# A half tile of tokens multiplied with one joint operand, and a reordered norm ahead of the first layer's routing

## The chip, the cores and the metric

The kernel runs on one core of a Trainium2 chip. The metric is device time in microseconds (us), the median of three runs. The core has five engines that run side by side, each through its own queue in order: TensorE (PE, with its weight loads shown as PEld), VectorE (DVE), ScalarE (ACT), GpSimd (POOL), and SyncE (SP), which here only starts DMA transfers. Matrix products land in PSUM, which has 8 banks of 512 float32 columns over 128 partitions.

## What is computed

Two layers of a hybrid backbone over 512 latent tokens (D = 1024) with 256 context tokens. Each layer has a token mixer (three parallel head groups, an output projection, a gated residual) and then a retrieval step (PEER). The change touches the seam between the two and the retrieval's last matrix product:

```python
x = x + g1 * yx                                   # output projection, gated residual
hx = rmsnorm(x, norm2_g[l]) * (1.0 + sc2) + sh2   # second norm
x = x + g2 * peer(hx, ...)

def peer(h, wq, keys, u_tab, v_tab):              # per token: 8 heads x top-16 of 128^2 experts
    q = (xb @ wq).reshape(T, PEER_HEADS, PEER_DQ)
    ...                                           # two top-k over 128 keys, one over 256 pairs
    gate = jax.nn.softmax(top_s, axis=-1)
    act = jax.nn.gelu(jnp.einsum('td,thkd->thk', xb, u_tab[eid]))
    return jnp.einsum('thk,thkd->td', gate * act, v_tab[eid])
```

The first layer also does all this for the context; the second does it for the latent tokens alone.

## The kernel before

The retrieval is done in two ways at once. **Dense**: for the first T latent tokens (T = 384 in the first layer, 320 in the second) all 16384 experts are computed. A u block (`ublock`) is 128 experts against T tokens, on PE, with a GELU on ACT into a slot of the SBUF tiles `PA` and `PB`. `weights` builds the sparse gate matrix by one-hot matmuls (`pwt`) and multiplies it into the slots. A v block (`vblock`, 128 per layer) multiplies a slot with 128 rows of `peer_v` and accumulates over all blocks in PSUM (`dacc0`, `dacc1`, ...). **Gathered**: for the other tokens (in the second layer 128 + 64, in the first 128 latent tokens and the 256 of the context) the rows of the chosen experts are fetched by an indirect DMA of POOL (`rows_of`, L1123), 128 rows of 1024 numbers at a time into one of five buffers `grow`, and DVE multiplies and adds each (L1134, L1147). There are 768 such gathers in the first layer and 384 in the second.

To keep the accuracy of float32, PE products are done in parts: an operand is split into a rounded part (`h`, a cast on ACT, L113) and the remainder (`l`, a subtraction on DVE, L114), and `mm` (L121) issues three passes. A v block loads its 128 x 1024 rows into a raw tile `uv` (three buffers in the second layer, shared with u blocks, two in the first), and splits them into `uvh` and `uvl` (two buffers each). The slot's columns are split into `wh` and `wl`.

T = 320 is two and a half tiles of 128 tokens. The half tile is not split: L1292 multiplies 64 float32 columns of the slot with the raw `uv`, one half of D into PSUM partitions 0 to 63 and the other into 64 to 127 of one bank, 64 of PE's columns each.

The order of the work on each engine is fixed when the kernel is built, by a planner that steps through a model of the machine: when an engine is idle in it, the ready instruction of the lowest level number goes next. `self.prio(n)` sets the level. The first layer's latent mixer and its retrieval have 3, the second layer's retrieval 5, all gathers 6, so that gathers fill what the rest leaves open on DVE. Within a level the order of the program text decides. On the chip each engine then works through its list in order and waits by semaphores.

At the seam, `back` runs the output projection tile by tile (`pwo`, two PSUM slots `S` of two banks), DVE scales and adds the residual (L610, L616), and SP stores the sum (L617). `transposed`, called by `route` (L944), squares and normalises a tile (L421, `rstd`, L423), transposes it by eight matmuls (`ptr`, L441, in one-bank slots `w`), scales it on the way out (L454, L456), and splits it into `dhT`. Then come the routing matmuls (`ppq`, `psc`) and the first u blocks (`pst`). In the first layer the pool that holds `ptr` is laid over banks of the projection's `S` slots; the transposes of the score maps in the mixer (`bpt`) use the last two banks.

Of the kernel before, what the change touches and what calls it, by code (L numbers as in the profile page):

```python
# [9 lines left out]
F32 = mybir.dt.float32  # L10
# [5 lines left out]
ALU = mybir.AluOpType  # L16
# [55 lines left out]
class Kern:  # L72
# [101 lines left out]
    def schedule(self):  # L174
        a = self.a
        with ExitStack() as er:
            ec = ExitStack()
            self.context(ec, 0)
            with self.banks("ctx0", "right", w=2, S=1) as ps, ExitStack() as e0:
                md = e0.enter_context(self.pool("mod", side="right"))  # L180
                pm = e0.enter_context(self.banks("mod", "right", w=1))
                fl = e0.enter_context(self.pool("flt"))
                pf = e0.enter_context(self.banks("flt", "left", w=2, S=1))
                with self.prio(1), ExitStack() as e:
                    self.filters(fl, pf, 0, LC)
                    self.modulation(md, pm, 0, 0, 2)
                    st = self.front(e, ps, ps, 0, 1, 1, side="right")
                    self.filters(fl, pf, 0, LX)
                    self.modulation(md, pm, 0, 2, 6)
                    self.back(ps, ps, 0, 1, st, None)  # L190
                    self.filters(fl, pf, 1, LX)
                    self.modulation(md, pm, 1, 0, 2)
            self.gp = er.enter_context(self.pool("gath", side="right"))
            with self.prio(1), self.banks("rc", "right", w=2) as ps:
                gc = self.route(ps, 0, 1, "GG", side="right")
            with self.banks("x0", "left", w=2, S=2) as ps:
                with ExitStack() as e:
                    with self.prio(3):
                        pr = e.enter_context(self.banks("x0b", "right", w=2))
                        st = self.front(e, ps, pr, 0, 0, 3, split=False)  # L200
                        ex, keep = ExitStack(), ExitStack()
                        rn = self.back(ps, pr, 0, 0, st, ex, keep=keep)
                        ex = (keep, ex)
                ec.close()
            with self.prio(6):
                self.gtile_u(0, gc[0])
                self.gtile_v(0, 1, 0, gc[0])
                self.gtile_u(0, gc[1])
            with self.prio(3):
                gx, ex = self.peer_x(0, 384, 31, 33, (36, 46, 46), ex, rn)  # L210
            with self.prio(6):
                self.gtile_u(0, gx[3])
                self.gtile_v(0, 0, 3, gx[3])
                self.gtile_v(0, 1, 1, gc[1])
            with ExitStack() as ec, ExitStack() as e:
                self.context(ec, 1)
                ps = e.enter_context(self.banks("x1", "left", w=2, S=2))
                pr = e.enter_context(self.banks("x1b", "right", w=2))
                with self.prio(3):
                    st = self.front(e, ps, pr, 1, 0, 4, ctx=True)  # L220
                with self.prio(4):
                    self.back(ps, pr, 1, 0, st, None, (2, 6))
            with self.prio(5):
                gx, _ = self.peer_x(1, 320, 32, 46, (44, 42, 42), (ex,))
            with self.prio(6):
                for i in sorted(gx, reverse=True):
                    self.gtile_u(1, gx[i])
                    self.gtile_v(1, 0, i, gx[i])
# [689 lines left out]
    def route(self, ps, l, s, kinds, hT=None, iT=None, i2n=None, side="left", done=(), fill=iter(()), rn=None,  # L918
# [10 lines left out]
        with ExitStack() as es:  # L929
# [10 lines left out]
            with nullcontext(rn) if rn else self.pool(f"rn{l}{s}", side=side) as sp:  # L940
                A2, B2 = rows or [sp.tile([128, D], F32, name=n) for n in ("A2", "B2")]
                nc.sync.dma_start(A2, bcast_rows(self.rows[l, 2, s, :]))
                nc.sync.dma_start(B2, bcast_rows(self.rows[l, 1, s, :]))
                for i, x in enumerate(self.transposed(sp, ps, l, 1, s, range(nt), hT, rest)):  # L944
                    if kinds[i] == "D":
                        continue
                    outs[i] = h = gp.tile([128, D], F32, name="ghx", bufs=2)
                    for dst, src in ((LO, HI), (HI, HI)) if kinds[i] == "H" else ((ALL, ALL),):
                        nc.vector.tensor_mul(h[dst], x[src], A2[src])
                        nc.vector.tensor_add(h[dst], h[dst], B2[dst])  # L950
# [233 lines left out]
    def peer_x(self, l, T, nA, nB, widths, done, rn=None):  # L1184
# [13 lines left out]
        with ExitStack() as es:  # L1198
# [74 lines left out]
                                                   1.0 / GSCALE, dst, op0=ALU.mult, op1=ALU.mult)  # L1273

            def vblock(i, sp):
                r0 = l * NEXP + i * 128
                if i in plain:
                    raw = dn.tile([128, D], F32, name="uv", bufs=2 + l)
                    nc.sync.dma_start(raw, a["peer_v"][r0:r0 + 128, :])
                    v, w = [raw], [slot(i)]  # L1280
                else:
                    raw, v = block("v", a["peer_v"][r0:r0 + 128, :])
                    w = [sp.tile([128, nd * 128], F32R, name=n, bufs=2) for n in ("wh", "wl")]
                    self.split(*w, slot(i)[:, :nd * 128])
                vh = [[x[:, h * 512:(h + 1) * 512] for x in v] for h in range(2)]
                for t in range(nd):
                    for h in range(2):
# [1 line left out]
                                [vh[h]], i == 0, i == 127)  # L1289
                if half:  # L1290
                    for h in range(2):
                        nc.tensor.matmul(acc[nd][h * 64:(h + 1) * 64], slot(i)[:, nd * 128:T],  # L1292
                                         raw[:, h * 512:(h + 1) * 512], start=(i == 0), stop=(i == 127))

            fill = (ublock(i) for i in range(nA))
            with self.banks(f"r{l}", "right", w=2, S=2) as ps:
                gx = self.route(ps, l, 0, "D" * nd + "H" * (nt - nd) + "G" * (4 - nt), hT, iT, i2n, "right", done, fill,
                                rn, [free[:, (i - 2) * D:nA * T + (i - 1) * D] for i in range(2)] if rn else None)
            for _ in fill:
# [2 lines left out]
            sp = ew.enter_context(self.pool(f"dw{l}"))  # L1302
            if nB:
                P.append(sp.tile([128, nB, T], F32, name="PB"))
            pa = es.enter_context(self.banks(f"da{l}", "left", w=nt - nd, S=nd))
            acc = [pa.S(f"dacc{i}") if i < nd else pa.w(f"dacc{i}") for i in range(nt)]
            due = {}
            for c, w in enumerate(widths):
                m0, m1 = cuts[c + 1] - R, cuts[c]
# [11 lines left out]
            if l == 0:  # L1321
                ex = ExitStack()
                self.res[0] = ex.enter_context(self.pool("xs1", side="right")).tile([128, 4, D], F32, name="xs")
            g2, fg, *rest = (free[:, i * D:(i + 1) * D] for i in range(2 + 2 * nt))
            nc.sync.dma_start(g2, bcast_rows(self.rows[l, 3, 0, :]))
            if l:
                nc.sync.dma_start(fg, bcast_rows(a["final_g"]))
# [3 lines left out]
            for t in range(nt):  # L1331
# [1 line left out]
                if t < nd:  # L1333
                    nc.vector.tensor_mul(y, acc[t], g2)
                else:
                    for h in range(2):
                        nc.vector.tensor_mul(y[LO, h * 512:(h + 1) * 512], acc[t][h * 64:(h + 1) * 64],
                                             g2[h * 64:(h + 1) * 64, h * 512:(h + 1) * 512])
                self.ended(dn, l, 0, t, ALL if t < nd else LO, y, res, res if l else self.res[0][:, t, :], fg)
        return gx, ex  # L1340

# [126 lines left out]
```

## Time and profile before

| | us |
|---|---|
| median of three runs (4218.82 to 4229.47) | 4218.94 |
| profiled execution | 4229.7 |
| its span, first to last instruction | 4227.9 |

Busy shares of the span: PE 88%, PEld 66%, DVE 83%, ACT 45%, POOL 37%. Each row of the views below is one execution on the chip, times from the start of the span. An engine's row in the order-of-time view gives start, duration, engine (a "q" for a queue that only issues), source line, operation, output <- inputs, shapes, how many were merged, and in brackets how long the engine was idle before and what it waited for. PE's durations overlap, since matmuls are pipelined: the step from one start to the next is what counts.

### The profile page before, as it was taken

Reading aid. Unit: us, or ns where it says so; the run is one execution under the profiler, and the core shown is the slowest. Engines: PE = TensorE matmul, PEld = TensorE weight load, DVE = VectorE, ACT = ScalarE, POOL = GpSimd, SP = SyncE. Lnnn points to the kernel's source line nnn. Section 1 sums busy time; section 2 is a strip of 40 time slices with the busy share of each in tenths; the row PEclk is TensorE's granted clock in tenths of the full one; section 3 lists DMA queues with packets and bytes.
Section 4 is the critical chain, followed back from the end, with each engine's and each line's share of the span. In section 5 each row is a group of like instructions: output and inputs, shape, how many; then the busy total and the mean of one; then the engine's idle time right before and its main releaser. Section 6 shows DMA issues by size and latency. Waiting matters only on the chain.

```text
span 4227.9 us, 63819 instructions
## 1 busy us (share of the span) xinstructions
PE 3702.5 (88%) x22532; PEld 2806.4 (66%) x22532; DVE 3509.9 (83%) x7455; ACT 1908.9 (45%) x3725; POOL 1543.7 (37%) x1225
## 2 busy tenths in 40 slices
PE   6987987967989999999979889888888999999997
PEld 3645544557878878877547666447788877776654
DVE  5746988888989989988999966645898998898988
ACT  5554343522347536633443344523334745555732
POOL 0000245642344573366447610000225345543243
PEclk7998998978999999999989989899989999999999
DMA  6655687875768897799989942333449888887797
GB/s 208 205 177 179 214 309 247 291 285 196 243 222 271 305 360 256 236 364 353 327 297 345 329 161 83 115 115 102 164 167 353 267 309 288 290 301 281 230 343 273
DMA packets 305634, 1063.74 MB, mean 252 GB/s; under 512 B 35756, under 2 KB 42624, under 8 KB 305314
## 3 DMA queue, kind: packets, MB, share of 16 engines
q0 software_dynamic: 165888, 604.05, 41.2%
q1 hardware_dynamic: 139426, 455.61, 30.7%
q8 instruction: 177, 2.90, 0.3%
q14 instruction: 143, 1.17, 0.1%
HBM read 1042.69 MB, written 16.84 MB: 251 GB/s over the span
## 4 chain that ended last, share of the span: by engine, by line
PE 35%; DMA 21%; DVE 18%; issue 15%; POOL 7%; ACT 5%; SPq 0%; POOLq 0%; DVEq 0%; ACTq 0%
PE pst L121 8%; PE dacc L121 7%; DMA grow<-in_peer_u_dram,eid 7%; POOL grow L1123 7%; DMA uv<-in_peer_v_dram 5%; PE pwin L121 4%; DMA uv<-in_peer_ut_dram 3%; DMA grow<-in_peer_v_dram,eid 3%; DVE uvl L114 2%; PE ppq L121 2%; DVE acc L1147 2%; DVE acc L1134 2%; PE fp L414 2%; PE pwo L121 2%; DMA wmod<-in_w_mod_dram 2%
## 5 line engine op out<-in xcount | busy, mean ns | idle before, releaser
L1123 POOL DMA_INDIRECT grow<-in_peer_u_dram,eid x576 | 753.9, 1309 | 1178.5 <-DVE acc L1134 599.3
L1123 POOL DMA_INDIRECT grow<-in_peer_v_dram,eid x576 | 782.1, 1358 | 700.5 <-DVE acc L1147 553.8
L121 PE MATMUL pst<-dhT,uvh 128*128 128x384 f32 (+1 forms) x4096 | 1001.9, 329 | 0.0
L121 PE MATMUL pst<-dhT,uvl 128*128 128x384 f32 (+1 forms) x2048 | 694.2, 339 | 118.9 <-DVE uvl L114 87.9
L113 ACT CAST uvh<-uv 128x1024 fp32r<-128x1024 f32 x494 | 516.5, 1046 | 622.1 <-DMA uv<-in_peer_v_dram 407.5
L1134 DVE SCALAR_TENSOR_TENSOR acc<-grow,ghx 128x1024 f32<-128x1024 f32 x576 | 703.1, 1221 | 76.1 <-DMA grow<-in_peer_u_dram,eid 71.1
L1147 DVE SCALAR_TENSOR_TENSOR acc<-grow,gate,acc 128x1024 f32<-128x1024 f32 x571 | 731.1, 1280 | 33.5 <-DMA grow<-in_peer_v_dram,eid 27.0
L121 PEld LDWEIGHTS pst<-dhT,uvh 128*128 128x128 f32 x4096 | 733.3, 193 | 1.5
L114 DVE TENSOR_TENSOR uvl<-uv,uvh 128x1024 fp32r<-128x1024 f32 x494 | 602.2, 1220 | 128.6 <-ACT uvh L113 125.1
L121 PEld LDWEIGHTS pst<-dhT,uvl 128*128 128x128 f32 x2048 | 395.7, 193 | 220.0 <-DVE uvl L114 164.0
L121 PE MATMUL dacc<-uvh,wl 128*128 128x512 f32 x1172 | 479.4, 409 | 16.2 <-DVE wl L114 11.4
L121 PE MATMUL dacc<-uvl,wh 128*128 128x512 f32 x1172 | 470.3, 401 | 18.1 <-DVE uvl L114 18.0
L121 PE MATMUL dacc<-uvh,wh 128*128 128x512 f32 x1172 | 464.7, 396 | 0.0
L1265 ACT ACTIVATE o<-iota,di2n 128x128 f16<-128x128 f16 x1056 | 325.3, 390 | 61.3 <-PE pwt L1269 61.2
L121 PEld LDWEIGHTS dacc<-uvh,wl 128*128 128x128 f32 x1172 | 221.1, 189 | 103.9 <-ACT wh L113 25.2
L121 PEld LDWEIGHTS dacc<-uvl,wh 128*128 128x128 f32 x1172 | 221.5, 189 | 72.1 <-DVE uvl L114 30.2
L121 PEld LDWEIGHTS dacc<-uvh,wh 128*128 128x128 f32 x1172 | 221.7, 189 | 49.2
L1269 PEld LDWEIGHTS <-o 128*128 128x128 f16 x4224 | 128.3, 97 | 111.4 <-issue 37.5
L1235 ACT ACTIVATE PA<-pst 128x320 f32<-128x320 f32 (+1 forms) x126 | 58.4, 463 | 293.6 <-PE pst L121 293.6
L1269 PE MATMUL pwt<-og,o 128*128 128x46 f16 (+3 forms) x4224 | 151.9, 183 | 36.9 <-DVE og L1255 31.9
L1235 ACT ACTIVATE PB<-pst 128x384 f32<-128x384 f32 (+1 forms) x130 | 60.1, 462 | 231.5 <-PE pst L121 231.0
L256 POOL MEMSET rmod<- 128x512 f32 (+1 forms) x8 | 3.3, 417 | 419.3 <-PE ptmod L282 169.2
(401 smaller groups left out, 6075.2 us busy)
## 6 DMA issues: line engine op xcount, KB each, us to landing
uv<-in_peer_ut_dram SPq DMA_DIRECT2D x256, 512.0 KB
uv<-in_peer_v_dram SPq DMA_DIRECT2D x256, 512.0 KB
wmod<-in_w_mod_dram SPq DMA_DIRECT2D x96, 512.0 KB
wpq<-in_peer_wq_dram SPq DMA_DIRECT2D x48, 512.0 KB
w_in<-in_w_in_dram SPq DMA_DIRECT2D x72, 256.0 KB
w_in<-in_w_in_dram SPq DMA_DIRECT2D x18, 512.0 KB
grow<-in_peer_u_dram,eid POOLq DMA_INDIRECT x576, 6.6
grow<-in_peer_v_dram,eid POOLq DMA_INDIRECT x576, 6.7
```

The source lines that it names most:

```text
L113: self.nc.scalar.copy(hi, src)
L114: self.nc.vector.tensor_tensor(lo, src, hi.bitcast(F32), op=ALU.subtract)
L121: self.nc.tensor.matmul(p, w[i], x[j], start=start and n == 0, stop=stop and n == len(passes) - 1)
L256: nc.gpsimd.memset(r, 0.0)
L414: self.nc.tensor.matmul(p, w, x, start=(i == 0), stop=(i == len(pairs) - 1))
L1123: self.nc.gpsimd.indirect_dma_start(out=r, out_offset=None, in_=self.a[table], in_offset=bass.IndirectOffsetOnAxis(ap=eid[:, j:j + 1], axi ...
L1134: nc.vector.scalar_tensor_tensor(junk, r, 1.0, hx, op0=ALU.mult, op1=ALU.mult, accum_out=dot[:, j:j + 1])
L1147: nc.vector.scalar_tensor_tensor(acc, r, w[:, j:j + 1], acc, op0=ALU.mult, op1=ALU.add)
L1235: nc.scalar.activation(slot(i), p, AF.Gelu_apprx_tanh)
L1265: nc.scalar.activation(o2[:, q], self.iota, AF.Abs, bias=i2n[:, t, k * NC + q:k * NC + q + 1])
L1269: nc.tensor.matmul(p[:, q, :], o2[:, q, :], og[:, g, q, :], start=(g == 0), stop=(g == 1))
```

## The change

1. **Half tile.** In `vblock`, `wh` and `wl` become one tile `both` of 2 T columns: the rounded part of all T columns, then the remainder, laid out so that the half tile's 64 rounded columns and its 64 remainder columns stand side by side. They are loaded as one operand of 128 columns, and multiplied with `uvl` and `uvh`, for each half of D: four matmuls with a full-width operand in place of two float32 ones with 64 columns. The remainder is made by two subtractions in the second layer (the half tile's 64 columns, then the other 256). `dacc2` takes two banks. At the end its upper 64 partitions are added to the lower ones, with one operation more on DVE. In the first layer (T = 384, no half tile) the same instructions stay.
2. **One slot less** in the second layer (`nB` 46 to 45), which pays for the larger tile.
3. **Order at the first layer's seam.** Each step of `transposed` runs at level 2 instead of 3 for the first layer's latent tokens.
4. **PSUM.** In `peer_x`, the routing's one-bank slots and its two-bank slots get pools of their own, so that the one-bank slots (`ptr`, `ppq`) lie on the last two banks and the two-bank ones (`psc`) on the four below.

```diff
-                gx, _ = self.peer_x(1, 320, 32, 46, (44, 42, 42), (ex,))
+                gx, _ = self.peer_x(1, 320, 32, 45, (44, 42, 42), (ex,))
...
-                for i, x in enumerate(self.transposed(sp, ps, l, 1, s, range(nt), hT, rest)):
+                tiles = enumerate(self.transposed(sp, ps, l, 1, s, range(nt), hT, rest))
+                while True:
+                    with self.prio(2) if l == 0 and not s else nullcontext():
+                        i, x = next(tiles, (nt, None))
+                    if i == nt:
+                        break
...
+                F = nd * 128
...
-                    w = [sp.tile([128, nd * 128], F32R, name=n, bufs=2) for n in ("wh", "wl")]
-                    self.split(*w, slot(i)[:, :nd * 128])
+                    both = sp.tile([128, 2 * T], F32R, name="w", bufs=2)
+                    w = [both[:, :F], both[:, 2 * T - F:]]
+                    nc.scalar.copy(both[:, :T], slot(i))
+                    for o, n, to in ((F, T - F, T), (0, F, 2 * T - F)):
+                        if n:
+                            nc.vector.tensor_tensor(both[:, to:to + n], slot(i)[:, o:o + n],
+                                                    both[:, o:o + n].bitcast(F32), op=ALU.subtract)
...
                 if half:
                     for h in range(2):
-                        nc.tensor.matmul(acc[nd][h * 64:(h + 1) * 64], slot(i)[:, nd * 128:T],
-                                         raw[:, h * 512:(h + 1) * 512], start=(i == 0), stop=(i == 127))
+                        for k in (1, 0):
+                            nc.tensor.matmul(acc[nd][:, h * 512:(h + 1) * 512], both[:, F:F + 128], vh[h][k],
+                                             start=(i == 0 and k == 1), stop=(i == 127 and k == 0))
...
-            with self.banks(f"r{l}", "right", w=2, S=2) as ps:
+            with self.banks(f"r{l}", "right", w=2) as ps, self.banks(f"rs{l}", "right", w=0, S=2) as big:
+                ps.S = big.S
...
-            pa = es.enter_context(self.banks(f"da{l}", "left", w=nt - nd, S=nd))
-            acc = [pa.S(f"dacc{i}") if i < nd else pa.w(f"dacc{i}") for i in range(nt)]
+            pa = es.enter_context(self.banks(f"da{l}", "left", w=0, S=nt))
+            acc = [pa.S(f"dacc{i}") for i in range(nt)]
...
-                    for h in range(2):
-                        nc.vector.tensor_mul(y[LO, h * 512:(h + 1) * 512], acc[t][h * 64:(h + 1) * 64],
-                                             g2[h * 64:(h + 1) * 64, h * 512:(h + 1) * 512])
+                    more = rest[2 * nt]
+                    nc.vector.tensor_mul(y[LO], acc[t][LO], g2[LO])
+                    nc.vector.tensor_mul(more[LO], acc[t][HI], g2[HI])
+                    nc.vector.tensor_add(y[LO], y[LO], more[LO])
```

## Rows read from the trace of the kernel before

**Rows 1.** Stretches: length, then busy us (instructions) by engine, clock, DMA share, GB/s.

```profile
865.00:903.00 38.00, 7.34 (x33) 5.19 (x31) 28.84 (x42) 17.24 (x40) 17.71 (x13) 0.55 0.84 310
...
4015.00:4202.00 187.00, 174.02 (x675) 100.85 (x673) 155.23 (x177) 58.26 (x83) 84.24 (x74) 0.99 0.94 338
...
3000.00:4202.00 1202.00, 1106.71 (x7703) 869.43 (x7702) 1073.76 (x2149) 600.97 (x1151) 511.64 (x384) 0.98 0.81 282
```

**Rows 2.** Order of time on PE, end of the first layer's projection to its routing.

```profile
864.81 1.04 PE L441 MATMUL ptr<-ident,xn 128*128 128x128 f32 x8
879.78 1.12 PE L441 MATMUL ptr<-ident,xn 128*128 128x128 f32 x4 [13.93 <-DVE hraw L454]
...
902.88 0.66 PE L121 MATMUL pst<-dhT,uvl 128*128 128x384 f32 x1 [2.43 <-DVE uvl L114]
```

**Rows 3.** Order of time on DVE in the same stretch.

```profile
875.82 1.22 DVE L610 TENSOR_TENSOR xs<-pwo,g 128x1024 f32<-128x1024 f32 x1
...
889.51 0.74 DVE L423 TENSOR_SCALAR xn<-xs,nry 128x1024 f32<-128x1024 f32 x1
...
901.52 1.22 DVE L114 TENSOR_TENSOR uvl<-uv,uvh 128x1024 fp32r<-128x1024 f32 x1
```

**Rows 4.** Order of time on SP's queue there: issues of DMA transfers.

```profile
863.42 16.34 SPq L617 DMA_DIRECT2D xsd<-xs  x2
...
881.35 1.10 SPq L1226 DMA_DIRECT2D uv<-in_peer_ut_dram  x2
```

**Rows 5.** Order of time on ACT there.

```profile
894.52 1.04 ACT L113 CAST uvh<-uv 128x1024 fp32r<-128x1024 f32 x1 [7.38 <-DMA uv<-in_peer_ut_dram]
```

**Rows 6.** Order of time on PE around one half tile of the second layer.

```profile
4060.51 0.40 PE L121 MATMUL dacc<-uvh,wh 128*128 128x512 f32 x1
4060.83 1.08 PE L1292 MATMUL dacc<-uv,PA 128*64 128x512 f32 x4
4061.84 0.50 PE L121 MATMUL dacc<-uvh,wl 128*128 128x512 f32 x1
4062.18 0.39 PE L121 MATMUL dacc<-uvl,wh 128*128 128x512 f32 x1
...
4064.48 0.39 PE L121 MATMUL dacc<-uvh,wh 128*128 128x512 f32 x1
```

**Rows 7.** The half tile's matmuls (L1292) in the last stretch, four a block.

```profile
4015.50:4202.00 186.50, 45.24 (x168) 8.22 (x168) 0.99 0.93 338
```

**Rows 8.** Waits of SP's queue, 3410 to 4202: in total, times, longest.

```profile
SPq L1226 <- PE dacc L1292: 327.0, 92, 6.2
```

**Rows 9.** Waits of PE in the same stretch.

```profile
PE pst L121 <- DVE uvl L114: 18.0, 17, 2.0
PE dacc L121 <- DVE uvl L114: 9.5, 15, 0.8
PE dacc L1292 <- DMA uv<-in_peer_v_dram: 5.1, 5, 2.1
```

**Rows 10.** Groups of instructions, shapes apart: busy us, mean ns | idle before.

```profile
L114 DVE TENSOR_TENSOR wl<-PB,wh 128x384 fp32r<-128x384 f32 x66 | 36.3, 551 | 0.0
L114 DVE TENSOR_TENSOR wl<-PA,wh 128x256 fp32r<-128x256 f32 x64 | 26.7, 418 | 0.4 <-ACT wh L113 0.3
```

**Rows 11.** DVE in stretches: gathers (L1147), then `uvl`, second layer; the same, first.

```profile
4059.20:4198.00 138.80, 71.48 (x56) 1.00 0.92 332
...
4059.20:4198.00 138.80, 37.96 (x31) 1.00 0.92 332
...
2213.70:2405.20 191.50, 107.58 (x85) 1.00 0.95 344
...
2213.70:2405.20 191.50, 51.33 (x42) 1.00 0.95 344
```

**Rows 12.** Gathers (L1147) in a dense run of them.

```profile
800.00:820.00 20.00, 14.77 (x12) 1.00 0.80 268
```

**Rows 13.** Order of time on DVE, the last gather of the kernel.

```profile
4210.22 1.26 DVE L1147 SCALAR_TENSOR_TENSOR acc<-grow,gate,acc 128x1024 f32<-128x1024 f32 x1
```

More of the change, by code (lines that the diff above doesn't have):

```diff
@@ L1323, in peer_x @@
                 self.res[0] = ex.enter_context(self.pool("xs1", side="right")).tile([128, 4, D], F32, name="xs")
-            g2, fg, *rest = (free[:, i * D:(i + 1) * D] for i in range(2 + 2 * nt))
+            g2, fg, *rest = (free[:, i * D:(i + 1) * D] for i in range(3 + 2 * nt))
             nc.sync.dma_start(g2, bcast_rows(self.rows[l, 3, 0, :]))
```

## The prediction

> **What bounds the kernel now.** I read the stretches first, then the order of time on each engine around the two edited places, then the waits, and the groups last for prices. The span has two places that the change touches. At the first layer's seam PE has almost nothing to do for 38.0 us: it is busy for 7.34, at a granted clock of 0.55 [rows 1]. The last tile's transposes come in between, after a wait of 13.93 for DVE, and the first product of the u blocks (`pst`) starts at 902.88 [rows 2]. In the second layer's dense part (3000 to 4202) PE is busy for 1106.71 of 1202.00 us and DVE for 1073.76 [rows 1]. So PE sets the pace there, with DVE close behind it. The reader is to see that both are near full: what one engine saves counts only as far as the other's list lets it.
>
> **First layer's seam: -6 us (-24 to +11).** Level 2 moves `transposed` among the projection's matmuls, and banks of their own let `ptr` start before `pwo`'s slots are read out. Nothing is added: 32 transposes, their scaling and their splits keep their durations. What comes next once they are early? On DVE the last residual sum runs at 875.82, and the last tile's norm ends its first step only at 889.51, 13.7 later [rows 3], which is the stretch that level 2 can close up. But `pst` also needs the first block of u. SP's queue issues the loads of `uv` at 881.35, behind the stores `xsd`, whose last issue waits for that residual sum [rows 4]; neither moves. ACT's cast waits for the load until 894.52 [rows 5] and takes 1.04, the subtraction `uvl` takes 1.22 [rows 3], so that `pst` can start at about 896.8 at best, where it now starts at 902.88 because `uvl` runs at 901.52, behind the read-outs of `ptr` and their splits. That is the 6. The best case, in which the loads move too, is 38.0 - 13.7 = 24. The worst: PE's list now has the transposes between the projection's products, and a transpose that waits for DVE's norm holds back the `pwo` matmuls queued behind it. DVE's last residual sum came 11.0 after PE's end of `pwo` (864.81 [rows 2] to 875.82 [rows 3]), so at worst DVE's lateness enters PE's queue whole, +11. The row nearest to this edit is the load's, so I take -6. The clock is low both before and after, and I count nothing for it.
>
> **Half tile on PE: -37 us (-37 to -12).** One half tile is four float32 matmuls. From the start of the first to the next matmul are 1.01 us, and the two steps around it are longer than others: 0.32 before (4060.51 to 4060.83) and 0.34 after, where the ten that follow take 2.30, 0.23 each [rows 6]. The whole is 0.32 + 1.01 + 0.34 = 1.67 for a stretch with two ordinary steps, 0.46, in it: 1.21 for the half tile. (The undisturbed block confirms it: one period is 4060.51 to 4064.48, 3.97, less 12 x 0.23 = 2.76, leaves 1.21.) The new form has four products with a full-width operand like the others, 4 x 0.23 = 0.92. The gain is 0.29 a block, 128 blocks: 37. If the longer steps around it stay, only 1.01 - 0.92 = 0.09 is gained, 12. I take 37, since the new operand has the form of its neighbours and those take 0.23.
>
> Four float32 matmuls in 1.01 are 0.25 each, hardly more than a rounded one. The Trainium skill, "TensorEngine Tiling (Array Packing)", Theoretical Speedup, says that operands of at most 64 columns can run side by side, up to twice as fast; that speaks against the change, which gives up this form. Did the pairs share PE wholly beyond what is measured, the half tile would cost about 0.50 and the joint operand would lose 0.42 x 128 = 54, an estimate from that page and the 1.01. The trace bears against it: the 1.01 already contains whatever overlap there is. The same page, Key Properties, says that a change of tiling mode drains PE; the longer steps of 0.32 and 0.34 agree with that.
>
> **Loads that start earlier: -26 us (-33 to 0).** Today the half tile reads the raw `uv`, so its buffer stays taken until PE has finished L1292. SP's queue, which issues the next load into it, waits for that 92 times, 327.0 us in all [rows 8]. Behind that wait stand the later loads of u and v, and behind those ACT's casts, DVE's `uvl` and PE. After the change the buffer is free once DVE has made `uvl`, before PE's block rather than at its end. PE's waits that hang on this are 18.0 + 9.5 for `uvl` and 5.1 for the load itself, 32.6 in all [rows 9]. What speaks against it: in the last stretch, 42 of the 128 blocks (168 matmuls of four a block), the DMA engines are 0.94 busy [rows 1], and a block takes 186.5 / 42 = 4.44 there [rows 7] against the undisturbed 3.97. An earlier issue into full queues lands hardly earlier. I keep four fifths of the 32.6, which is 26; the ends are all of it and nothing.
>
> **DVE's work and the gathers it pushes back: +52 us (0 to +85).** DVE gets one more subtraction a block, of 64 columns. The 384-column one takes 551 ns, the 256-column one 418 [rows 10]: 133 for 128 columns, so 0.066 for 64 columns and 418 - 266 = 152 for each instruction, 0.22 together, 28 us in 128 blocks. ACT's cast is longer by 64 columns, which its idle time hides. DVE is covered by nothing: it has 1202.00 - 1073.76 = 128 us idle, and its list is filled by the planner, which puts gathers where its model leaves DVE open. How does the model price PE? In the first layer a block has 18 products, and DVE has 1.22 (`uvl`, 51.33 / 42), 0.55 (`wl` [rows 10]) and 85 / 42 = 2.02 gathers of 1.27 in it [rows 11]: 4.34 to 4.36 a block, 0.242 for each product. In the second a block has 12 and the half tile, and DVE has 1.22 + 0.42 + 56 / 31 = 1.81 gathers of 1.28 [rows 11], 3.96; less 12 x 0.242 = 2.90 leaves 1.06 as its price of the half tile. The new one is 4 x 0.242 = 0.97. So the model's block is shorter by 0.09 and has 0.22 more of DVE's other work: 0.31 / 1.28 = 0.24 gathers fewer, 31 in 128 blocks. They come after the dense part, where no matrix product is left to hide them. A dense run of gathers goes at 20 / 12 = 1.67 each [rows 12], so they cost 52. Today there is nearly no such tail: the last gather starts at 4210.22 [rows 13], 8 us behind the dense part's end at 4202. Ends: none, if DVE's idle time takes them all; 85, if the model's block shrinks by the real 0.29 (below).
>
> **The rest: 0.** The slot less moves one block's u part earlier in the order; its work is the same. The final stage has one more addition and wider multiplications for the half tile, two or three us of DVE by the 1.22 of a full-width sum [rows 3]; the pushed-back gathers cover it, as the half tile's result isn't wanted until they end. If there is no tail, 2 to 3 us show.
>
> **Sum.** -6 - 37 - 26 + 52 = -17. The profiled execution took 4229.7 with a span of 4227.9, 10.8 above the median of 4218.94, 0.26%. I take the 17 from both: 4213 profiled, **4202 us** for the median.
>
> **The rivals.** *A, slower: the gathers' stream takes the end.* If the planner credits the joint operand with the whole 0.29, a block loses (0.29 + 0.22) / 1.28 = 0.40 gathers, 51 in all, 85 us of tail. The sum is -6 - 37 - 26 + 85 = +16, 4235. It decides from 41 gathers on, at which the tail (41 x 1.67 = 69) eats the gain of 69. For it: DVE's 89% busy share, and that total DVE work grows. Against it: the price of 1.06 read from rows 11. *B: loads start no earlier in effect.* The DMA share of 0.94 and DVE's list set the dense pace, the 26 are lost: +9, 4228. For it: the 4.44 a block in the last stretch. Against it: 327.0 us of SP's waits in a stretch of 792. *C: the seam closes whole.* -24 in place of -6, because SP's order moves too: 4184. Against it: the stores' place ahead of the loads [rows 4]. *D: the longer steps stay around the joint operand.* -12 in place of -37: +8, 4227. *E: level 2 doesn't move the transposes,* because DVE's order, not the level, holds them: 0 in place of -6, 4208.
>
> **How the numbers follow.** Chances: forecast 0.46, A 0.15, B 0.20, C 0.11, D 0.04, E 0.04. A measurement of this kernel can tell about 0.3% from no change, 12.7 us: below 4206.3 is faster, above 4231.6 slower. The forecast's own range is 4185 to 4222 (25 to 43 gathers, loads between -33 and -13). It lies below 4206.3 in two thirds of its cases, 0.31, and within 0.3% in 0.15. C adds 0.11 to faster, and a few points come from B and D with fewer gathers than reckoned: 0.46. Same gets 0.15, most of B (0.14), D, E: 0.34. Slower is A and the rest of B with more gathers: 0.20. The range reaches from C with a tail of 20 gathers (4184 less 18, and some more for an unpushed order: 4160) to A with the loads half lost and no seam gain (4242).
>
> **What would show it.** Seam: `ptr` of the first three tiles stand between `pwo`'s matmuls, and `pst` starts before 897, with `uvl` right behind its cast. Half tile: all steps 0.23, a block in 3.68 undisturbed. Loads: SP's waits name DVE's `uvl` in place of PE's L1292, and PE's 32.6 shrink. Gathers: some 31 of them behind the dense part's end; 51 would be A, a handful would make it faster than forecast by up to 50 us. I am wrong if blocks stay at 4.4 though PE's steps are 0.23 (then DVE or the DMAs set the pace), or if the projection's matmuls show waits for the norm.

## The result: 60 us faster, where 17 were forecast

| | before | after |
|---|---|---|
| median, us | 4221.86 | 4161.95 |
| ratio, with its 95% interval | | 0.9857 (0.9835 to 0.9878) |
| profiled execution, us | 4229.7 | 4165.2 |
| its span, us | 4227.9 | 4163.4 |

A second set of runs of the changed kernel (e9 below) gave 0.9873 (0.9848 to 0.9898). The direction was right, the size was not: 60 us are three and a half times the 17 of the forecast, though the time lies inside the wide range of 4160 to 4242.

By the order-of-time views of the two profiled executions, the 64.5 us between the spans lie here (starts of the first `pst`, end of the last `dacc` product, end of the span):

| stretch | before | after | change |
|---|---|---|---|
| start to the first layer's first `pst` | 902.9 | 897.6 | -5.3 |
| from there to the second layer's first `pst` | 2003.1 | 1999.1 | -4.0 |
| the second layer's dense part, to the last `dacc` | 1297.1 | 1214.9 | -82.2 |
| from there to the end | 24.8 | 51.8 | +27.0 |

The -4.0 is nothing to explain. The projection's first product, ahead of which no edit acts, started anywhere from 795.7 to 814.8 us in the profiles of this case, so single profiles differ by as much.

**The dense part.** Stretches of the kernel before and after, with columns as in [rows 1]: the dense part from its first v block on, then the stretch behind the last weights ([rows 1] has 4015 to 4202 of before), then the tail.

```profile
3427.00:4202.00 775.00, 736.99 (x4529) 516.63 (x4528) 677.85 (x990) 382.49 (x712) 350.16 (x253) 0.99 0.85 298
```

```profile
3406.00:4111.00 705.00, 695.63 (x4553) 591.97 (x4552) 679.88 (x1109) 382.14 (x714) 337.91 (x244) 1.00 0.89 319
...
3950.00:4111.60 161.60, 159.86 (x688) 127.09 (x686) 156.51 (x227) 58.70 (x85) 103.83 (x72) 1.00 0.99 370
4111.60:4163.00 51.40, 0.04 (x1) 0.00 (x0) 39.27 (x48) 6.92 (x13) 17.31 (x12) 0.53 0.57 191
```

The reader is to see three things. PE was idle for 38.0 of 775 us and is now for 9.4 of 705. The DMA engines' share in the last stretch went from 0.94 to 0.99 and their rate from 338 to 370 GB/s, so the loads had room. And behind the dense part there is now a tail of 51.4 us in which PE does nothing.

**The half tile.** One block of after on PE, in order of time (columns as in [rows 6]):

```profile
4058.63 0.39 PE L121 MATMUL dacc<-uvh,w 128*128 128x512 f32 x1
4058.86 0.39 PE L1306 MATMUL dacc<-uvl,w 128*128 128x512 f32 x1
4059.09 0.39 PE L1306 MATMUL dacc<-uvh,w 128*128 128x512 f32 x1
4059.31 0.39 PE L1306 MATMUL dacc<-uvl,w 128*128 128x512 f32 x1
4059.54 0.40 PE L1306 MATMUL dacc<-uvh,w 128*128 128x512 f32 x1
4059.78 0.40 PE L121 MATMUL dacc<-uvh,w 128*128 128x512 f32 x1
...
4062.54 0.39 PE L1306 MATMUL dacc<-uvl,w 128*128 128x512 f32 x1
```

The four products are 0.23 apart and so are their neighbours; the block takes 4062.54 - 4058.86 = 3.68, as forecast, against the 3.97 of [rows 6]. The long steps around the float32 half tile are gone, which agrees with what the prediction quoted of the Trainium skill, "TensorEngine Tiling (Array Packing)", Key Properties: no change of tiling mode is left in the block, every product has 128 by 128. That such changes made the long steps is not shown: in e4 below all products have 128 by 128 too, and the step after a float32 one is 0.31 all the same (4107.63 to 4107.94).

**The loads.** Waits in the dense part, before (3427 to 4202) and after (3406 to 4111): in total, times, longest.

```profile
ACT uvh L113 <- DMA uv<-in_peer_v_dram: 119.7, 57, 4.4
DVE uvl L114 <- ACT uvh L113: 78.5, 65, 3.3
ACT uvh L113 <- DMA uv<-in_peer_ut_dram: 55.2, 34, 3.1
...
SPq L1226 <- DVE uvl L114: 151.2, 63, 7.3
```

```profile
DVE uvl L114 <- ACT uvh L113: 7.0, 22, 0.7
...
ACT uvh L113 <- DMA uv<-in_peer_v_dram: 6.1, 2, 3.1
...
ACT uvh L113 <- DMA uv<-in_peer_ut_dram: 1.4, 1, 1.4
...
SPq L1231 <- DVE uvl L114: 536.3, 155, 5.9
```

SP no longer waits for PE (327.0 in [rows 8]), ACT's casts hardly wait for loads any more (174.9 in all, now 7.5), and DVE hardly for the casts (78.5, now 7.0).

### The profile page after: what moved, and what is told of

Its sections match the earlier page's. It is cut to its first block, busy times and chain, and to the rows that moved or that the text cites. A ratio compares the mean times of both kernels' runs of the same rounds, so it can differ in the third digit from the quotient of the medians.

```text
span 4163.4 us, 64129 instructions
## 1 busy us (share of the span) xinstructions
PE 3651.6 (88%) x22532; PEld 2873.5 (69%) x22532; DVE 3527.2 (85%) x7584; ACT 1906.8 (46%) x3725; POOL 1535.8 (37%) x1225
## 4 chain that ended last, share of the span: by engine, by line
PE 38%; DVE 19%; DMA 18%; issue 15%; POOL 6%; ACT 4%; SPq 0%; POOLq 0%; DVEq 0%; ACTq 0%
PE pst L121 9%; PE dacc L121 8%; DMA grow<-in_peer_u_dram,eid 7%; POOL grow L1128 6%; DMA grow<-in_peer_v_dram,eid 4%; PE pwin L121 4%; DMA uv<-in_peer_v_dram 3%; PE ppq L121 3%; DVE acc L1152 2%; DVE uvl L114 2%; DVE acc L1139 2%; PE pwo L121 2%; PE pwt L1274 2%; PE fp L414 2%; PE dacc L1306 1%
## 5 line engine op out<-in xcount | busy, mean ns | idle before, releaser
L121 PE MATMUL dacc<-uvh,w 128*128 128x512 f32 x2344 | 783.6, 401 | 14.2 <-DVE w L1296 13.1
L121 PEld LDWEIGHTS dacc<-uvh,w 128*128 128x128 f32 x2344 | 443.2, 189 | 120.7 <-DVE w L1296 22.6
L121 PE MATMUL dacc<-uvl,w 128*128 128x512 f32 x1172 | 470.2, 401 | 12.1 <-DVE uvl L114 11.7
L121 PEld LDWEIGHTS dacc<-uvl,w 128*128 128x128 f32 x1172 | 221.8, 189 | 63.9 <-DVE uvl L114 20.9
L121 PE MATMUL pwin<-hT,w_inh 128*128 128x256 f32 (+1 forms) x576 | 146.8, 346 | 0.7 <-DVE hT L114 0.7
L113 ACT CAST wpqh<-wpq 128x256 fp32r<-128x256 f32 x192 | 75.7, 406 | 148.5 <-PE ppq L121 94.0
```

Of the source, the lines that this page charges most:

```text
L113: self.nc.scalar.copy(hi, src)
L121: self.nc.tensor.matmul(p, w[i], x[j], start=start and n == 0, stop=stop and n == len(passes) - 1)
```

## The experiments

All ratios are to the kernel before, run on the same chip as the experiment; chips differ, so ratios are compared, not times. A remark on the texts on record: where they count 30 and 16 gathers behind the dense part, a second record of the same line was counted with each gather. The profile's groups have 16 and 9 there, and 2 in the kernel before.

| run | what it is | ratio | interval |
|---|---|---|---|
| e1_half | half tile and slots alone | 0.9891 | 0.9869 to 0.9914 |
| e2_seam | level and banks alone | 0.9981 | 0.9968 to 0.9994 |
| e3_freed | before, raw buffer free early | 0.9876 | 0.9857 to 0.9895 |
| e4_held | after, raw buffer held | 1.0020 | 1.0005 to 1.0035 |
| e5_buf4 | before, four raw buffers | 0.9925 | 0.9906 to 0.9944 |
| e6_dup | after, one subtraction | 0.9849 | 0.9832 to 0.9867 |
| e7_order | level alone | 1.0008 | 0.9992 to 1.0024 |
| e8_banks | banks alone | 0.9957 | 0.9937 to 0.9977 |
| e9_after | after, again | 0.9873 | 0.9848 to 0.9898 |
| e10_nolevel | after without the level | 0.9861 | 0.9835 to 0.9886 |
| e11_nolevel_dup | e10 with one subtraction | 0.9852 | 0.9824 to 0.9880 |
| e12_two | after, two raw buffers | 1.0104 | 1.0073 to 1.0135 |
| e14_four | e10 with four raw buffers | 0.9860 | 0.9830 to 0.9891 |
| e15_freed_sub | e3 with a subtraction more | 0.9912 | 0.9883 to 0.9941 |
| e16_freed | e3, again | 0.9885 | 0.9856 to 0.9915 |

**The two halves of the change.** e1 keeps the seam as before, e2 the half tile (each is the diff with the other part undone).

> The kernel before with the half tile's joint operand alone (points 1 and 2 of the change); the seam's order and banks stay as before. Changed kernel: -60 us by the median. Theory 'the second layer holds nearly all of it': -48 to -56, the dense part shorter by about 82 us from the first pst to the last dacc, some 30 gathers behind its end. Rival 'the new banks carry part of the second layer's gain' (its routing stretch became 12 us shorter before any v block began): -35 to -45, and the routing stretch from the first pst to the first dacc keeps its 521 us.

> The kernel before with points 3 and 4 alone: level 2 for the first layer's norm and transposes, pools of their own for the routing's banks. Theory 'seam only': the first pst at about 897.6 instead of 902.9 and the end 5 to 6 us earlier, -5 to -9 by the median. Rival 'the banks also speed up the second layer's routing': -15 to -20, with the second layer's stretch from first pst to first dacc some 10 us shorter.

Measured: -46 us (0.0109 x 4222) and -8 us. They add up to -54, within the scatter of the whole. The second layer holds nearly all of it, though -46 lies between the two cases of e1, just short of its theory's range, and 16 gathers lie behind its dense part. The stretch that both rivals named, from the second layer's first `pst` to its first `dacc` product, is 513.7 us in e2 and 513.3 in e1, against 521.5 before and 509.5 after. But it is 515.5 in e3, which has neither half of the change, so it tells nothing of the banks; and the -15 to -20 of e2's rival did not come. Its dense part, from the start of the first `pst` to that of the last `dacc` product, is 1291.7 us against 1296.5, no more than profiles scatter.

**The held buffer alone.** e3 leaves PE's and DVE's work in the form of before and changes only what the half tile reads (it is a probe and no substitute, since it leaves out the remainder of v there); e4 does the opposite to the changed kernel.

```diff
-     raw[:, h * 512:(h + 1) * 512], start=(i == 0), stop=(i == 127))
+     v[0][:, h * 512:(h + 1) * 512].bitcast(F32), start=(i == 0), stop=(i == 127))
```

```diff
+ ...                                              # zero: a tile of 128 x 128, set to 0 once
+     if h > k:
+         nc.tensor.matmul(acc[nd][:, 512:514], zero, raw[:, 512:514], start=False, stop=False)
```

> The kernel before, in which the half tile's float32 matmuls multiply the rounded part uvh in place of the raw uv, so that the raw buffer is free after the split; PE's work and DVE's work keep their form. The remainder of v is left out for the half tile. Theory 'loads': the gain beyond the 38 us of PE's steps (about 44 us) is due to the raw buffer being held, so this gains -30 to -44, DVE's idle time before uvl falls from 86 us to under 30, and blocks without u stay at 3.97 at best but average close to it (4.0 in place of 4.44). Rival 'PE's steps': all of it came from the shorter half tile, and freeing the buffer alone gives -5 to +3.

> The changed kernel with one small matmul more in each v block of the second layer: a zero operand times two columns of the raw uv, added to dacc2 ahead of the last product, so that the raw buffer is held until PE is nearly through the block, as before the change. Theory 'loads': it gives back 30 to 45 us, 4192 to 4207, with SP waiting for PE and blocks without u at 4.1 to 4.4 on average. Rival 'PE's steps': only the small matmul's own time, up to 0.1 us a block, 0 to +13, 4162 to 4175.

Measured: -52 us for e3 (0.0124 x 4222), and -49 in its repetition e16. That is more than the -30 to -44 of the theory: freeing the buffer early brings as much as the whole of e1, with no shorter half tile at all. e4 is 0.0147 above e9, and 0.0148 above what e1 and e2, run on its chip, give together (0.9872): 62 us, more than either of its cases. Its small product costs more than was allowed for:

```profile
4107.49 0.28 PE L1310 MATMUL dacc<-uv,zero 128*128 128x2 f32 x2
4107.63 0.47 PE L1311 MATMUL dacc<-uvh,w 128*128 128x512 f32 x1
4107.94 0.39 PE L121 MATMUL dacc<-uvh,w 128*128 128x512 f32 x1
...
4111.38 0.28 PE L1310 MATMUL dacc<-uv,zero 128*128 128x2 f32 x2
```

This order of time on PE in e4 gives a block of 4111.38 - 4107.49 = 3.89, 0.21 over the 3.68 of after, 27 us in 128 blocks. So some 35 of e4's loss are left for the held buffer, within the 30 to 45 of the theory, and PE's idle time in the dense part is 37.6 us against the 9.4 of after. The waits of e3 (3435 to 4165) and of e4 (3430 to 4203) bear out the mechanism in both directions:

```profile
DVE uvl L114 <- ACT uvh L113: 7.3, 19, 0.4
...
SPq L1226 <- DVE uvl L114: 471.8, 138, 5.4
```

```profile
DVE uvl L114 <- ACT uvh L113: 63.1, 55, 3.4
...
SPq L1234 <- PE dacc L1311: 327.7, 96, 6.3
```

**How many raw buffers.** e5 gives the kernel before a fourth (three slots less); e12 takes the changed kernel's third away; e14 gives a fourth to the changed kernel without the level.

```diff
- raw = dn.tile([128, D], F32, name="uv", bufs=2 + l)
+ raw = dn.tile([128, D], F32, name="uv", bufs=2 + 2 * l)      # e5, e14; e12: bufs=2
```

> The kernel before with four raw buffers uv in the second layer in place of three, paid for by three slots (46 to 43); the half tile still multiplies the raw uv in float32. Theory 'the held buffer': freeing the buffer after the split brought 51 us in the dense part without any other edit, and one buffer more lengthens the ring from three blocks to four, so that SP's wait for PE hides: -40 to -55, DVE's idle time before uvl under 20 us. Rival 'SP's order': every load behind a waiting one is late all the same, since SP's queue is worked off in order; the fourth buffer only shifts the wait: -5 to -25.

> The changed kernel with two raw buffers uv in the second layer in place of three. Theory 'what counts is that the buffer is free after the split, a block before PE': a load (issue to cast 8.5 us now, much of it waiting for its turn on ACT) still fits in two blocks' time, +5 to +20 against the changed kernel. Rival 'the number of loads under way counts': as bad as the held buffer, +40 or more.

> The changed kernel without level 2, with four raw buffers uv in the second layer in place of three, paid for by three slots (45 to 42). Theory 'three suffice once the buffer is free after the split' (PE is idle for only 9 of 705 us): within 8 us of the same without the fourth (0.9861). Rival 'the ring still costs': 10 us or more faster, 0.983 or less. Slower by more than 8 would be the price of the slots.

Measured: -32 for e5, between its two cases. DVE's idle time before `uvl` fell to 28.2, not under 20, and 7 gathers came to lie behind the dense part. The half tile's matmuls (L1292, L1306), four a block, behind the last weights, 42 blocks each, in e3, e5, e12 and after (columns as in [rows 7]):

```profile
3997.50:4164.80 167.30, 45.31 (x168) 8.30 (x168) 1.00 0.97 365
```

```profile
4017.50:4185.50 168.00, 45.30 (x168) 8.30 (x168) 1.00 0.97 359
```

```profile
4015.50:4196.50 181.00, 46.88 (x168) 31.28 (x167) 0.98 0.91 324
```

```profile
3952.30:4107.70 155.40, 46.66 (x168) 30.69 (x169) 1.00 0.99 374
```

A block takes 3.98 in e3, 4.00 in e5, 4.31 in e12 and 3.70 in after, where it took 4.44 before [rows 7]. So in this stretch the fourth buffer brings what freeing the buffer early brings. What e5 lacks lies ahead of it: from the second layer's first `pst` to the last weights it gains 13 us and e3 31. Whether the alternation of u and v blocks or the three slots less are the reason stays open.

e12 is worse than the kernel before by 44 us and than e9 by 97: the rival holds, against my theory. ACT's casts wait for loads in it for 232.0 us (3422 to 4200):

```profile
ACT uvh L113 <- DMA uv<-in_peer_v_dram: 189.4, 57, 8.1
...
DVE uvl L114 <- ACT uvh L113: 85.6, 74, 3.7
...
ACT uvh L113 <- DMA uv<-in_peer_ut_dram: 42.6, 28, 3.4
```

A fourth buffer for the changed kernel brings nothing (0.9860 against 0.9861). Three suffice once they are free early.

**DVE's time and the gathers.** e6 and e11 write the half tile's rounded columns a second time on ACT, so that one subtraction of 320 columns does; e15 adds a subtraction of 64 columns to e3.

```diff
- both = sp.tile([128, 2 * T], F32R, name="w", bufs=2)
- ...                                              # the two subtractions
+ both = sp.tile([128, 3 * T - F], F32R, name="w", bufs=2)
+ w = [both[:, 2 * T - F:], both[:, :T]]
+ self.split(*w, slot(i))
+ if T > F:
+     nc.scalar.copy(both[:, T:2 * T - F], slot(i)[:, F:])
```

> The changed kernel with one subtraction of 320 columns in place of two (256 and 64); the half tile's rounded columns are written a second time by ACT, beside the remainder, so that the operand of 128 columns still stands in one piece. ACT gets one cast of 64 columns more a block. Theory 'VectorE's time sets how many gathers are left behind the dense part': about 0.15 us less on DVE a block, 19 us, so some 15 gathers fewer behind the end of the dense part (15 in place of 30) and 12 to 20 us faster than the changed kernel: 4142 to 4150 where that gives 4162. Rival 'PE alone sets the dense part and ACT's cast holds it': -3 to +8 against the changed kernel.

> As the last, with the single subtraction of 320 columns and ACT's second cast for the half tile's columns. With level 2 that left 16 gathers behind the dense part in place of 30 and gained 3 us of some 15 expected. Theory 'the gathers brought forward cost in the dense part what they save behind it': within 6 us of the run without it. Rival 'the earlier profile was a slow one': 10 to 18 us faster than the run without it.

> The kernel before with the half tile in float32 from uvh (raw buffer free after the split; the remainder of v is left out for the half tile), and one more subtraction of 64 columns on DVE in each v block, whose result nobody reads. Theory 'DVE's added time pushes gathers out': 0.22 / 1.28 x 128 = 22 gathers behind the dense part, where the run without it has none, and 15 to 28 us slower than that run. Rival 'DVE's idle time takes it': the same number behind it, within 5 us.

> The kernel before with the half tile in float32 from uvh (the remainder of v is left out for the half tile), again, beside the last on one chip: 0.986 to 0.990 of the kernel before.

Measured: e15 is 13.5 us slower than e16 by the medians (4193.4 and 4179.9; 0.0027 by the ratios), just under the range given. Behind its dense part 11 gathers lie, where e16 has none, by the gathers' line (L1147) on DVE in the two tails:

```profile
4152.10:4192.60 40.50, 13.36 (x11) 0.55 0.52 172
```

```profile
4159.20:4178.30 19.10, 0.00 (x0) 0.58 0.26 82
```

So one more small subtraction does push gathers out, with PE's work unchanged. e6 goes the other way, 9 in the tail (16 in after), and gains nothing that can be told (0.9849 against 0.9857 and 0.9873; e11 0.9852 against e10's 0.9861): the rival of no gain. Its tail is 12 us shorter and its dense part, 1226.1 us by the same two starts, 12 longer than that of after (1214.5). e11 repeats it against e10: a tail 11 shorter, a dense part 11 longer (1222.4 and 1211.5). The other profiles of the changed kernel's dense part, 1215.4 in e9 and 1220.3 in e1, lie below both, so gathers that are brought forward cost there about what they save behind, as far as so few profiles tell.

**The seam's two edits apart.**

> The kernel before with point 3 alone (level 2 for the first layer's norm and transposes), the banks as before. Points 3 and 4 together: -8 us (ratio 0.9981). Theory 'the level moves the work, the banks matter little': -4 to -8, ptr between the projection's matmuls. Rival 'the banks are needed': ptr lies over banks of the projection's slots, so that a transpose put early waits for a read-out of pwo and holds PE's queue: -2 to +10.

> The kernel before with point 4 alone (pools of their own for the routing's one-bank and two-bank slots), levels as before. Theory 'the level moves the work': within 3 us of the kernel before. Rival 'the banks carry it': -5 to -9, as with both.

> The changed kernel again, beside the next three on one chip, so that they are compared with it directly: 0.984 to 0.988 of the kernel before.

> The changed kernel without level 2: half tile, slots and banks as changed, the first layer's norm and transposes at the same level as the rest of the mixer. Theory 'the banks carry the seam's gain and the level gives part of it back' (banks alone 0.9957, both 0.9981, level alone 1.0008): 5 to 11 us faster than the changed kernel, first pst 92 to 93 us behind the first pwo. Rival 'the two are the same, the difference was between runs' (first pst 92.5 behind the first pwo with the banks alone, 93.5 to 94.5 with both): within 3 us of the changed kernel.

Measured: the level alone is nothing (1.0008), the banks alone -18 us (0.9957), more than the two together, though the intervals of e2 and e8 overlap. The order of time on PE in e8 and e7:

```profile
796.76 1.12 PE L121 MATMUL pwo<-wo,cat 128*128 128x512 f32 x2
...
886.28 1.94 PE L441 MATMUL ptr<-ident,xn 128*128 128x128 f32 x8 [3.83 <-DVE xn L423]
889.23 0.69 PE L121 MATMUL pst<-dhT,uvl 128*128 128x384 f32 x1 [1.01 <-DVE uvl L114]
```

```profile
805.71 1.13 PE L121 MATMUL pwo<-wo,cat 128*128 128x512 f32 x2
...
815.18 50.91 PE L121 MATMUL pwo<-wo,cat 128*128 128x512 f32 x118
865.93 1.04 PE L441 MATMUL ptr<-ident,xn 128*128 128x128 f32 x8
...
905.19 0.66 PE L121 MATMUL pst<-dhT,uvl 128*128 128x384 f32 x1 [2.44 <-DVE uvl L114]
```

From the projection's first product to the first `pst` are 92.5 us with the banks and 99.5 with the level alone, where before has 98.3 and after 93.5. Over all profiles it is 91.3 to 95.0 in the four with the banks and not the level, 92.6 to 95.8 in the six with both, and 95.6 to 103.0 in the six with neither. So the seam accounts for 6 of e8's 18 us; its profile starts the projection 8 us earlier than that of before, ahead of any edit, and does not place the rest. In e7 all transposes (`ptr`) stay behind all of `pwo`'s products, as before. That the changed kernel is better without the level could not be told: e10 is 5 us ahead of e9 by the medians (4160.4 and 4165.2), inside both intervals. No run beats the changed kernel by more than its interval.

## Why the prediction was wrong, step by step

**Seam, -6: right in size and place, wrong in what does it.** e2 gave -8. The bound was the load, as forecast: ACT's cast and then DVE's `uvl` in after, with the PE line that waits for them.

```profile
895.24 1.04 ACT L113 CAST uvh<-uv 128x1024 fp32r<-128x1024 f32 x1 [5.38 <-DMA uv<-in_peer_ut_dram]
```

```profile
896.31 1.23 DVE L114 TENSOR_TENSOR uvl<-uv,uvh 128x1024 fp32r<-128x1024 f32 x1 [5.39 <-ACT uvh L113]
```

```profile
840.31 1.40 PE L441 MATMUL ptr<-ident,xn 128*128 128x128 f32 x8 [4.12 <-DVE xn L423]
841.50 12.72 PE L121 MATMUL pwo<-wo,cat 128*128 128x512 f32 x26
...
884.16 1.12 PE L441 MATMUL ptr<-ident,xn 128*128 128x128 f32 x4 [11.90 <-DVE hraw L454]
...
897.59 0.69 PE L121 MATMUL pst<-dhT,uvl 128*128 128x384 f32 x1 [10.12 <-DVE uvl L114]
```

`uvl` now follows its cast at once (in [rows 3] it came at 901.52, seven behind [rows 5]). The transposes do move among `pwo`'s products, and one of them waits 4.12 us there, as the bad case had it. But only two of the four tiles' transposes move (840.31 and 854.06), and `pst` starts at 897.59, not before 897. It is the banks that bring the gain, with all transposes behind `pwo` (e8); the level alone moves nothing on PE and gains nothing (e7), and with the banks its moves add nothing (e10). I had read the two as one edit.

**Half tile on PE, -37: the steps were right, and two thirds of the time came.** Block 3.68, steps 0.23. Behind the last weights the whole gain is there, 3.98 a block in e3 and 3.70 in after. Between e3 and e1, which both have early loads, the dense part shrinks by 25.6 us (1245.9 to 1220.3), and 16 gathers left it. Where the other 11 us stay no run shows.

**Loads, -26: the first of two terms that failed.** By e3 and e16 it is -52 and -49, beyond the end of -33 that I gave as "all of it". The mechanism was right and the price was read from the wrong row: the waits of PE that name `uvl` or a load [rows 9]. They are 32.6 us; PE's whole idle time in the stretch is 38.0; and with the same 4527 or so products PE is busy for 736.99 us before and 722.44 in e3:

```profile
3435.00:4165.00 730.00, 722.44 (x4527) 512.66 (x4527) 683.63 (x993) 382.81 (x712) 335.10 (x253) 1.00 0.89 317
```

So 14.6 us of the loss stood inside "busy". The granted clock, 0.993 and 0.998 over the two stretches, accounts for at most 0.005 x 737 = 4 of them. For the others there was a row that the prediction did not read, the waits of PE's weight loads, while products still run:

```profile
PEld pst L121 <- DVE uvl L114: 46.1, 32, 2.9
```

With the rows that name `uvh` and the load, PEld waits for 85.0 us in before and for 15.2 in e3: more than the gain, where PE's own waits are less. A better row was in the prediction and went unused: a block takes 4.44 in the last stretch and 3.97 undisturbed [rows 7, 6], and 0.47 x 128 = 60 is near the 51, the dense part's difference between before and e3 (1296.5 and 1245.9). It is near by an average: e3 gains 19.4 us, 0.45 a block, in the 43 blocks behind the last weights, and 0.37 a block ahead of them. I had argued that DMA engines at 0.94 would leave no room. They went to 0.99 and the block to 3.70, so that argument fell with rival B.

The raw buffers are used in turn, as a ring. One buffer's way round it in before shows where the 4.44 comes from (SP's issue, the first of the two in the first row, then ACT's cast, DVE's subtraction, PE's half tile of the same block, SP's next issue into the buffer):

```profile
4105.56 4.30 SPq L1226 DMA_DIRECT2D uv<-in_peer_v_dram  x2
...
4118.84 0.33 SPq L1226 DMA_DIRECT2D uv<-in_peer_v_dram  x1
```

```profile
4112.63 1.05 ACT L113 CAST uvh<-uv 128x1024 fp32r<-128x1024 f32 x1 [2.63 <-DMA uv<-in_peer_v_dram]
```

```profile
4113.71 1.23 DVE L114 TENSOR_TENSOR uvl<-uv,uvh 128x1024 fp32r<-128x1024 f32 x1 [1.24 <-ACT uvh L113]
```

```profile
4117.72 1.08 PE L1292 MATMUL dacc<-uv,PA 128*64 128x512 f32 x4
```

From issue to issue are 13.28 us for three buffers (13.3 in the mean over the loads behind the last weights), 4.43 a block: the ring, not PE, set the pace. Freed at `uvl`'s end (4114.94), the same way is 9.38, 3.13 a block, below PE's 3.68 or 3.97; with two buffers it would be 4.69, above it. This is one way round, with its waits in it, so it tells on which side of PE's step a ring lies and not the exact pace. In that it agrees with e12 (4.31 a block), e3 (3.98) and e14, and with e5 behind the last weights: 13.28 / 4 = 3.32, and a block takes 4.00, close to PE's own 3.97. Ahead of them e5 got less than the ring would allow.

**Gathers, +52: the second term that failed; the number of them was twice too high, the price right.** The tail grew by 27.0, and 16 gathers lie in it against 2. Less some 2.4 for the wider final stage (an estimate, two operations of 1.22), 24.6 / 14 = 1.76 each, where I took 1.67. The 31 came from adding durations. DVE's instructions overlap by nearly 0.1, and the step counts:

```profile
4072.78 0.42 DVE L114 TENSOR_TENSOR wl<-PA,wh 128x256 fp32r<-128x256 f32 x1
4073.11 1.22 DVE L114 TENSOR_TENSOR uvl<-uv,uvh 128x1024 fp32r<-128x1024 f32 x1
```

```profile
4103.30 0.55 DVE L1296 TENSOR_TENSOR w<-PB,w 128x64 fp32r<-128x64 f32 x2
4103.77 2.60 DVE L1152 SCALAR_TENSOR_TENSOR acc<-grow,gate,acc 128x1024 f32<-128x1024 f32 x2
```

The Trainium skill, "Perfetto Trace Analysis", Summary: the profiler window per engine type, says that a record of DVE runs until its write is acknowledged; the overlap of 0.09 (4072.78 + 0.42 against 4073.11) agrees with that.

In before (first fence) the subtraction takes 0.33 of DVE's time, in after the pair takes 0.47: 0.14 more, not 0.22. That alone is 0.14 x 128 = 18 us, 14 gathers by their duration of 1.28 and 15 by their step of 1.20 (the median in after from 3960 to 4100, where the next instruction follows at once), against the 14 found; for the 0.09 that I read into the planner's price nothing is left. By the same count e6's single subtraction, whose step is 0.40 there, saves 0.07 x 128 / 1.20 = 7 gathers, and 7 fewer lie in its tail. The number does not hang on DVE's work alone, though: e5 adds none and has 7, where e3 has none.

**The sum again.** In the profiles the seam gives -5, the loads -51 (e3), the half tile -26 (e1 against e3) and the tail +26 (e1 against before), where -6, -26, -37 and +52 were forecast: the forecast was too slow by some 25 us in the loads and again in the gathers, and too fast by 11 in the half tile. Half tile and gathers together were forecast at -37 + 52 = +15; e1 against e3 gives +6 (0.0015, with some 0.003 of uncertainty), the traces -25.6 in the dense part and +32 behind it. So, as far as that uncertainty lets it be told, the joint operand's saving on PE goes into the gathers that it and its subtraction push back; what it buys on balance is that the raw buffer is free early. -8, -51 and +6 make -53, against -54 and -60 measured. The rivals: A has the true mechanism of the tail, but at 14 gathers, far from its turning point of 41; B, C and D fell; of E, the half on the level holds: alone, it moves no transpose.

## What to carry to other kernels

Price a stall by the period of the repeated unit against its undisturbed period, not by the waits that name the suspect: here the latter gave 33 us on PE and 85 on its weight loads, the former 60, and the truth was 51. Where a ring of buffers feeds a loop, add up one buffer's way round (load, casts, the last reader) and divide by the number of buffers; if that exceeds the loop's step on its busiest engine, the last reader is what to move, and a faster last reader is worth less than an earlier one (e4 has the faster one alone, e3 the earlier one alone). On a full engine, cost an added instruction by the step to the next start, not by its duration.

## What the runs showed of the hardware

Two raw buffers instead of three cost 97 us, with each buffer freed by DVE as in after: ACT waited 232.0 us in that dense part for loads of 512 KB, up to 8.1 at a time. A float32 product of two columns with a zero operand cost PE 0.21 us a block, about as much as a whole 512-column product in rounded form (0.23): 0.14 to the next product, whose own step was then 0.31 in place of 0.23. Why, no run shows.
